# New key scores that wait longer for a page visit, and side jobs handed to PE with slack, in a planned decoder step

## The chip, the cores and the metric

The kernel runs on one core of a Trainium2 chip. The metric is the device time of one execution in microseconds (us). Before the change three runs took 855.38, 855.73 and 856.23 us; the median is 855.73. Engines are named as in the profile: PE is TensorE, PEld its weight load, DVE is VectorE, ACT is ScalarE, POOL is GpSimd, and SP is SyncE, which issues most DMA transfers.

## The reference

One decoder layer is computed in float32 for a prompt of 256 tokens and for 8 requests of 8 new tokens each, with 2048 cached tokens per request. One projection of the 320 rows feeds three groups of heads, and each group's output is multiplied by its own SiLU gate before the output projection and a LayerNorm:

```python
z = jnp.einsum('btd,dn->btn', h, w)          # one projection, cut into 13 parts
# A: sparse attention, 8 heads x 128: an indexer scores all keys, the best 256 or fewer are attended
s = jnp.einsum('bthd,btkhd->bthk', q, k_sel) * (DH_A ** -0.5)
# B: gated linear recurrence, 4 heads: S_t = diag(f_t) S_{t-1} + (1 - f_t) outer i_t, o_t = S_t^T q_t
# M: cross attention, 4 heads x 128, into 256 memory tokens per request
s = jnp.einsum('bthd,bnhd->bhtn', q, mk) * (DH_M ** -0.5)
y = jnp.einsum('btn,nd->btd', cat, w_out)
return _layernorm(ALPHA * h + y, ln_g, ln_b)
```

The cached keys and values lie in pages of 128 tokens, which a page table finds. The requests are handled in four pairs, p = 0 to 3; the keys of the 8 new tokens of each request are attended too.

## The kernel before, in words

**The matmuls.** Weights and activations are split into a high and a low part that PE multiplies at its fast float32 rate, so each product of a projection takes three matmuls (`xh` with `wh`, `xl` with `wh`, `xh` with `wl`). ACT casts the high part `wh` of a weight tile, DVE or POOL subtracts to get the low part `wl` (`prep`). A quantum of a projection is six matmuls. The projections (`wspec`, in the order of `PROJECTIONS`) run through the whole kernel; the memory projection is one of them; the output projection (`wo`) comes last.

**Page visits.** Keys and values come in units of two pages for each request of a pair. A visit (`unit`, line 722 and on) multiplies one or two units: `kv` rows are key scores with `qpad` as weights, `va` rows are values with the transposed probabilities `PT`. The weights of these matmuls have 32 columns, those of the projections 128. `units_now` takes two units together when the second is loaded too, and a single one when no projection part is about to be ready.

**Side jobs.** Everything else that PE does is in small generators in the list `bg`: attention scores, transposes, the recurrence (`hgrn`), the probabilities' transposes, cross attention (`cross_prompt`, line 1317). A generator stops at `yield need(...)`, which lists the tiles that it needs next, how many PSUM buffers (`ps`, 1 unless said), a `lag` and, for jobs whose weights have 32 columns too, a time `visit` that it may wait for a page visit. With `ps=0` the next step is not one of PE. There are three kinds of job with a visit time: the scores of the new tokens' own keys (`new_keys`, line 1201: `akS` with `qpad`, one job for each pair p), the recurrence's level scores (`kk, q, *lv`, time `HASTE`), and the state times queries of the decode part (`S0, q`, time `VISIT_WAIT`).

**The planner.** The order of all instructions is made when the program is built. `Plan` keeps, for each engine, the time up to which it is planned, and for each tile the time from which it can be read; each operation has a cost (`Engine.cost`) and each engine a latency. The loop at the end of the kernel (line 2115) goes on with the planned time `plan.now`: loads are issued on SP, weight parts prepared, finished projections evacuated, and `background` (line 2021) resumes side jobs whose needs are met. Then PE gets either a visit or a quantum of projection. `met` tells whether the tiles are ready: readable at `plan.now` or earlier, `lag` included. A job with a visit time is not resumed by `background` until that time has passed since it was first met; `join_visit`, called right behind a visit, resumes those that are met.

The engines execute what was put in their queues in that order, and wait on semaphores where a tile is not ready in reality. A planned time is no time of the chip, and none is used here.

Before the change the lines are:

```python
def need(*aps, ps=1, lag=0.0, visit=0.0):
    return (aps, ps, lag, visit)
...
        yield need(akS, st["qpad"], visit=VISIT_WAIT)
```

All operations are recorded by one helper, line 157, so the profile's rows are told apart by their tiles: `mB<-akS,qpad` are new key scores, `mB<-bp` level scores, `mA<-bp,t` with 128 columns out the decode state, `m.<-ident,t` transposes, `t<-t,s` of DVE the scaling of cross attention's probabilities.

Of the kernel before, what the change touches and what calls it, by code (L numbers as in the profile page):

```python
# [41 lines left out]
SOON = 0.4  # L42
LAG = 1.5
LAG2 = 0.8
VISIT_WAIT = 9.0
HASTE = 2.0
CALM = 4.0
# [172 lines left out]
        return (66 + n * f) / 960 + 0.055 * scalars  # L220


def need(*aps, ps=1, lag=0.0, visit=0.0):

    return (aps, ps, lag, visit)


@with_exitstack
def hymba_step(ctx: ExitStack, tc: tile.TileContext, I, O):
    nc = tc.nc  # L230
    plan = Plan()
    PE, ACT, DVE, POOL, SP = (Engine(plan, n, e) for n, e in (
        ("PE", nc.tensor), ("ACT", nc.scalar), ("DVE", nc.vector), ("POOL", nc.gpsimd), ("SP", nc.sync)))
# [22 lines left out]
    def free(*ts):  # L256
        for t in ts:
            e = live.get(t.tensor.name)
            if e:
                e[1] -= 1  # L260
                if e[1] == 0:
                    del live[t.tensor.name]
# [8 lines left out]
    def const(shape, name, dt=F32):  # L271
        return pool.tile(shape, dt, name=name, tag=name, bufs=1)

    def T(cols=NT, dt=F32):
        return new([128, cols], "t", dt)

    def T8():
        return new([128, 8], "s8")
# [9 lines left out]
    def n_free(which):  # L288
        return min(plan.n_free(which, 2), 2 - held[which])


    def PS(shape, which=None, dt=F32):
        if which is None:
            fa, fb = [(held[w] == 2, plan.slot_free(w, 2)) for w in ("mA", "mB")]
            which = "mA" if fa <= fb else "mB"
        return new(shape, which, dt, psum)
# [27 lines left out]
    akS = const([128, 8, NS], "akS")  # L324
# [26 lines left out]
    st = {}  # L351
# [101 lines left out]
    def pad_queries():  # L453
        yield from wait(("mq", 0))
        yield from room(1, "bp")
        st["mqpad"] = x = new([128, 8, 4, 32], "bp")
        POOL.memset(x, 0.0)
        for h in range(4):
            yield from wait(("mq", h))
            q = st.pop(("mq", h))  # L460
            yield need(q, ps=0)
            ACT.copy(x[:, :, h, 8 * h:8 * h + 8], q[:, 256:320].rearrange("p (b t) -> p b t", b=8))
            free(q)
        done.add("mqpad")
# [11 lines left out]
    def cat_put(c, part, cols, src, eng=None):  # L476
        out = cat_tile(c)[:, cols]
        if src.ndim > 2:
            out = out.rearrange("p (b q) -> p b q", b=src.shape[1])
        cat_left["p" if part == "p" else "s", c] -= 1  # L480
        if (c, part) in cat_seen:
            DVE.tensor_mul(out, out, src)
        else:
            cat_seen[c, part] = 1
            (eng or DVE.tensor_copy)(out, src)
# [17 lines left out]
    def gate(c, gates):  # L503
        for g, t in sorted(gates.items()):
            yield need(t, ps=0)
            cat_put(g, "p", slice(0, 256), t[:, 0:256])
            if g < 12:
                cat_put(g, "s", slice(256, 320), t[:, 256:320])
            else:
                for q in range(2):  # L510
                    s = slice(256 + 32 * q, 288 + 32 * q)
                    cat_put(g, ("s", q), s, t[:, s])
            free(t)
        done.add(("gate", c))
# [207 lines left out]
    def unit(n):  # L722
# [4 lines left out]
        if kind == "K":  # L727
# [12 lines left out]
            if u % 2:  # L740
                ps = st.pop("kv")
                plan.pinned.add(ps.tensor.name)
                bg.insert(0, [key_scores(p, u, ps), need(ps, ps=0)])
# [85 lines left out]
    def wait(*keys):  # L829
        while not all(k in done for k in keys):  # L830
            yield
# [85 lines left out]
    def idx_sample():  # L917
# [103 lines left out]
        for k, (sp, c, f, a) in enumerate(steps):  # L1021
            n = kk[0].shape[-1]
            yield need(ql, qh, *kk, ps=2, lag=LAG2)
            pd = [PS([128, 512]), PS([128, 512])]
# [176 lines left out]
    def new_keys(p):  # L1201

        yield from wait(("ak", 7))
        while p not in S:
            yield
        yield need(akS, st["qpad"], visit=VISIT_WAIT)
        ps = PS([128, NS])
        for hh in range(2):
            for h2 in range(2):
                for b, hp, g in GROUPS:  # L1210
                    h = 4 * hh + 2 * hp + h2
                    PE.matmul(ps[g:g + 32, :], st["qpad"][:, h, 2 * p + b, :], akS[:, h, :], start=hh == h2 == 0,
                              stop=hh == h2 == 1)
        plan.pinned.add(ps.tensor.name)
        yield need(ps, ps=0)
        plan.pinned.discard(ps.tensor.name)
        ACT.activation(S[p][:, PAST:], ps, AF.Copy, scale=QS)
        done.add(("new", p))
# [98 lines left out]
    def cross_prompt(h):  # L1317
        yield from wait("mem", ("mq", h), "attn")
        yield need(MQ[h], st["mkT"][h])
        ps = PS([128, 2, 256])  # L1320
        for tt in range(2):
            PE.matmul(ps[:, tt, :], MQ[h][:, 128 * tt:128 * tt + 128], st["mkT"][h], start=True, stop=True)
        s8 = T8()
        DVE.tensor_reduce(s8[:, 0:2], ps, axis=AX.X, op=OP.max)
        DVE.tensor_scalar(s8[:, 2:4], s8[:, 0:2], -QS, None, op0=OP.mult)
        free(MQ.pop(h), st["mkT"][h])
        P = [T(256), T(256)]
        yield need(s8, ps=0)
        for tt in range(2):
            ACT.activation(P[tt], ps[:, tt, :], AF.Exp, bias=s8[:, 2 + tt:3 + tt], scale=QS,  # L1330
                           accum_out=s8[:, 4 + tt:5 + tt])
        yield need(P[1], ps=0)
        DVE.reciprocal(s8[:, 6:8], s8[:, 4:6])
        for tt in range(2):
            DVE.tensor_scalar(P[tt], P[tt], s8[:, 6 + tt:7 + tt], None, op0=OP.mult)
        yield need(*P)
        pt = PS([128, 2, 2, 128])
        for nt in range(2):
            for tt in range(2):
                PE.transpose(pt[:, nt, tt, :], P[tt][:, 128 * nt:128 * nt + 128], ident)  # L1340
        free(*P)
        pts = [T(256), T(256)]
        for nt in range(2):
            ACT.copy(pts[nt], pt[:, nt].rearrange("p a b -> p (a b)"))
        yield need(*pts)
        po = PS([128, 256])
        for nt in range(2):
            PE.matmul(po, st["mv"][nt][h // 2][:, 128 * (h % 2):128 * (h % 2) + 128], pts[nt],
                      start=nt == 0, stop=nt == 1)
        cat_put(12 + h, "p", slice(0, 256), po, ACT.copy)  # L1350
        free(*pts)
        if h % 2:
            for nt in range(2):
                free(st["mv"][nt][h // 2])
# [10 lines left out]
    def hgrn():  # L1365
        lb, olb = lbt[:, 8:12], lbt[:, 12:16]
        yield from wait("idxdone", "pbias", "masks")
        for h in range(4):
# [184 lines left out]
            free(S2)  # L1553
            yield need(S0, q, visit=VISIT_WAIT)
            pq = PS([128, 2, 128])
# [457 lines left out]
    for g in (setup(), masks(), idx_head(), idx_sample(), attn_scores(), attn_values(), *[new_keys(p) for p in range(4)],  # L2013
              *[soft(p) for p in range(4)], hgrn(), pad_queries(), *[cross_prompt(h) for h in range(4)], split()):
        bg.append([g, None])
# [5 lines left out]
    def background():  # L2021
        rank = {"idx_load": 0, "idx_sample": 1, "idx_prompt": 1, "attn_scores": 2, "hgrn": 1, "xsoft": 1,
                "xextract": 1, "extract": 1, "key_scores": 0, "split": 1, "soft": 0, "attn_values": 1}
        for e in sorted(bg, key=lambda e: rank.get(e[0].__name__, 2)):
            for _ in range(4):
                if max(plan.t["DVE"], plan.t["ACT"]) > plan.now + (4, 3.5, 2)[int(rank.get(e[0].__name__, 2))]:
                    break
                if e[1]:
                    if not met(e[1]):
                        break  # L2030
                    if e[1][3] and nunit < len(punits) and plan.now < asked.setdefault(e[0], plan.now) + e[1][3]:
                        break
                if not resume(e) or e[1] is None:
                    break

    asked = {}

    def met(want):
        deps, nps, lag, _ = want
        return all(plan.avail(a) + lag <= plan.now for a in deps) and (not nps or n_free("mA") + n_free("mB") >= nps)  # L2040

    def resume(e):
        asked.pop(e[0], None)
        try:
            e[1] = next(e[0])
        except StopIteration:
            bg.remove(e)
            return False
        return True

    def join_visit():

        for e in list(bg):
            if e[1] and e[1][3] and met(e[1]):
                resume(e)

    def loads():
# [57 lines left out]
    while half < len(wspec) or bg or outq or later_in or pending or nunit < len(punits):  # L2115
        plan.now = max(plan.now, plan.t["PE"])
        loads()
        if pending and pending[0][0] is mem_values and has_room(4, spare=spare()):
            f, ps, _ = pending.pop(0)
# [8 lines left out]
        while pending and plan.avail(pending[0][1] if pending[0][2] == 3 else pending[0][1][-1]) <= plan.now \  # L2128
# [3 lines left out]
            f, ps, _ = pending.pop(0)  # L2132
# [139 lines left out]
```

## Time and profile before

| what | value |
|---|---|
| median of three runs | 855.73 us (855.38 to 856.23) |
| the profiled execution's own time | 855.43 us |
| its span, first to last instruction | 853.7 us |
| mean granted TensorE clock | 0.998 |
| HBM read | 256.50 MB |

The profile's first part gives the busy time of each engine and its share of the span, with the count of instructions. The list of waits names the engine and output tile that waited, who ended the wait, the time in total, how often, and the longest. In the timeline a row is the start, the time to the end of the row, the engine, the line, the operation with its output and inputs, the shape and the count; idle time of the engine ahead of it stands in brackets. Matmuls overlap in the timeline, so what one costs is the distance from its start to the next start. Some matmuls of float32 weights are recorded twice, once for each pass.

### The profile page before, as it was taken

How to read it: one execution, taken by the hardware profiler on the slowest of the kernel's cores; microseconds unless marked ns; L12 is line 12 of the kernel's file. 1: busy time of each engine (PE TensorE's matmuls, PEld its weight loads, DVE VectorE, ACT ScalarE, POOL GpSimd, SP SyncE). 2: the span in 40 equal slices, each digit the busy share in tenths (PEclk: the TensorE clock that was granted, in tenths of full speed). 3: DMA queues.
4: the chain of work that ended last, by engine and by line, in shares of the span. 5: the costliest groups of instructions: out<-in, count | busy, mean ns of one | idle time of the engine just before them, and what ended most of it. 6: DMA issues, size and time to landing. Idle time of an engine off the chain costs nothing.

```text
span 853.7 us, 19146 instructions
## 1 busy us (share of the span) xinstructions
PE 844.3 (99%) x6889; PEld 719.0 (84%) x6892; DVE 553.8 (65%) x1100; ACT 422.0 (49%) x908; POOL 325.4 (38%) x333
## 2 busy tenths in 40 slices
PE   9999999999999999999999999999999999999996
PEld 8999999877889898878778788787886889888885
DVE  7888897744897898654474456558545343953655
ACT  6454565553555543634544554555444353744432
POOL 0677562565634445331141214333311110713424
PEclk9999999999999999999999999999999999999999
DMA  8567557889999999999989999999999988756633
GB/s 342 171 190 226 158 172 253 281 308 412 375 388 395 336 322 366 398 367 399 390 321 412 407 352 393 398 370 412 338 411 396 350 329 285 279 172 199 195 99 123
DMA packets 83216, 266.49 MB, mean 312 GB/s; under 512 B 10481, under 2 KB 21170, under 8 KB 82482
## 3 DMA queue, kind: packets, MB, share of 16 engines
q1 hardware_dynamic: 82098, 263.18, 83.4%
q0 software_dynamic: 1024, 2.10, 0.8%
q8 instruction: 54, 0.88, 0.4%
q14 instruction: 40, 0.33, 0.1%
HBM read 256.50 MB, written 8.73 MB: 311 GB/s over the span
## 4 chain that ended last, share of the span: by engine, by line
PE 98%; DVE 1%; ACT 0%; issue 0%; DVEq 0%
PE pj L157 56%; PE mB L157 13%; PE va L157 10%; PE mA L157 10%; PE kv L157 8%; PE kv L1947 0%; DVE pg L157 0%; DVE t L157 0%; ACT t L157 0%; DVE wl L157 0%; DVE s L157 0%; DVEq L2258 0%; ACT wh L157 0%; DVE avn L157 0%; ACT kN L157 0%
## 5 line engine op out<-in xcount | busy, mean ns | idle before, releaser
L157 ACT CAST wh<-wr 128x512 fp32r<-128x512 f32 x334 | 204.5, 619 | 246.0 <-PE pj L157 186.8
L157 PE MATMUL pj<-xh,wh 128*128 128x320 f32 (+1 forms) x992 | 313.7, 316 | 0.0
L157 PE MATMUL pj<-xh,wl 128*128 128x320 f32 (+1 forms) x992 | 303.9, 306 | 0.0
L157 PE MATMUL pj<-xl,wh 128*128 128x320 f32 (+1 forms) x992 | 303.9, 306 | 0.0
L157 DVE TENSOR_TENSOR wl<-wr,wh 128x512 fp32r<-128x512 f32 x222 | 172.8, 786 | 183.4 <-ACT wh L157 169.6
L157 POOL TENSOR_TENSOR wl<-wr,wh 128x512 fp32r<-128x512 f32 x112 | 150.7, 1354 | 239.6 <-ACT wh L157 216.4
L157 PEld LDWEIGHTS pj<-xh,wh 128*128 128x128 f32 x992 | 186.7, 188 | 16.8 <-issue 13.0
L157 PEld LDWEIGHTS pj<-xl,wh 128*128 128x128 f32 x992 | 186.8, 188 | 1.3
L157 PEld LDWEIGHTS pj<-xh,wl 128*128 128x128 f32 x992 | 186.6, 188 | 0.0
L157 POOL TENSOR_TENSOR t<-t,t 128x256 f32<-128x256 f32 (+3 forms) x53 | 46.0, 869 | 121.3 <-ACT t L157 60.1
L157 PE MATMUL va<-pg,PT 128*32 128x512 f32 x456 | 58.4, 595 | 0.0
L157 PE MATMUL kv<-pg,qpad 128*32 128x256 f32 (+1 forms) x916 | 57.5, 380 | 0.0
L157 PEld LDWEIGHTS kv<-pg,qpad 128*32 128x32 f32 (+1 forms) x916 | 30.9, 110 | 20.5 <-issue 1.3
L157 PEld LDWEIGHTS va<-pg,PT 128*32 128x32 f32 x456 | 14.6, 109 | 30.4 <-issue 28.4
L157 DVE MAX8 PT<-PT 128x8 f32<-128x1032 f32 x32 | 39.5, 1234 | 0.5
L157 DVE MATCH_REPLACE8 PT<-PT 128x1032 f32<-128x1032 f32 x32 | 39.0, 1218 | 0.0
L157 POOL DMA_INDIRECT S<-in_ci,row x24 | 25.6, 1065 | 20.0 <-DVE row L157 10.5
L157 PE MATMUL mB<-t,wh 128*128 128x256 f32 x128 | 24.5, 289 | 0.0
L157 POOL TENSOR_TENSOR bp<-t,bp 128x128 f32<-128x128 f32 (+1 forms) x17 | 10.6, 625 | 36.0 <-ACT bp L157 36.0
L157 DVE TENSOR_TENSOR cat<-S,cat 64x512 fp32r<-64x512 f32 x24 | 19.2, 802 | 7.4 <-ACT cat L157 6.9
L157 POOL TENSOR_TENSOR t<-t,tabm 128x320 f32<-128x320 f32 x16 | 14.5, 906 | 24.4 <-DVE t L157 24.2
L157 POOL TENSOR_TENSOR xl<-cat,xh 128x256 fp32r<-128x256 f32 x12 | 12.5, 1060 | 24.9 <-ACT xh L157 24.9
(430 smaller groups left out, 1355.2 us busy)
## 6 DMA issues: line engine op xcount, KB each, us to landing
wr<-in_wt SPq DMA_DIRECT2D x124, 512.0 KB, 5.4
pg<-in_ck SPq DMA_DIRECT2D x114, 512.0 KB, 7.3
pg<-in_cv SPq DMA_DIRECT2D x114, 512.0 KB, 8.0
wr<-in_wo SPq DMA_DIRECT2D x36, 512.0 KB, 4.4
wr<-in_wm SPq DMA_DIRECT2D x16, 512.0 KB, 7.0
S<-in_ck SPq DMA_DIRECT2D x14, 512.0 KB, 6.5
S<-in_cv SPq DMA_DIRECT2D x14, 512.0 KB, 7.1
pg<-in_cXV SPq DMA_DIRECT2D x8, 512.0 KB, 8.1
```

The source lines that it names most:

```text
L157: res = f(*a, **k)
```

## The change: what it does

It adds a constant and changes five places:

```diff
+SLACK = 0.3
...
-def need(*aps, ps=1, lag=0.0, visit=0.0):
+def need(*aps, ps=1, lag=None, visit=0.0):
-    return (aps, ps, lag, visit)
+    return (aps, ps, lag if lag is not None else SLACK if ps and not visit else 0.0, visit)
...
-        yield need(akS, st["qpad"], visit=VISIT_WAIT)
+        yield need(akS, st["qpad"], visit=2 * VISIT_WAIT)
...
-        yield need(*P)
+        yield need(*P, lag=1.2)
         pt = PS([128, 2, 2, 128])
...
-    def met(want):
+    def met(want, now=None):
         deps, nps, lag, _ = want
-        return all(plan.avail(a) + lag <= plan.now for a in deps) and (...)
+        return all(plan.avail(a) + lag <= (now or plan.now) for a in deps) and (...)
...
     def join_visit():
         for e in list(bg):
-            if e[1] and e[1][3] and met(e[1]):
+            if e[1] and e[1][3] and met(e[1], max(plan.now, plan.t["PE"] - 0.4)):
                 resume(e)
```

A side job that needs PE and states neither a lag nor a visit time now gets a lag of 0.3: its tiles must have been readable for 0.3 us of planned time before PE is given the job. The transposes of the cross attention's probabilities `P` get 1.2. New key scores wait up to 18 instead of 9 us of planned time for a visit. And a visit takes the jobs whose tiles are readable 0.4 us before its own planned end, where before they had to be readable at its start. No operation is added or taken away by hand; all else that moves, moves because the planner places it otherwise. The order holds 5581 matmuls before and after.

Three places of the new order follow. The helper's line is 158 in the changed kernel.

On PE, the new key scores of pair p = 2; `pj` is a projection, `kv` a key visit, `cat,avn` the values of the prompt's attention. Before:

```order
L157 MATMUL pj_4217<-xh,wh_4204 128x320
L157 MATMUL pj_4217<-xl,wh_4204 128x320
L157 MATMUL pj_4217<-xh,wl_4205 128x320
L157 MATMUL mB_4309<-akS,qpad_411 32x64 x16
L157 MATMUL pj_4217<-xh,wh_4204 128x320
```

After:

```order
L158 MATMUL kv_4377<-pg_4247,qpad_411 32x256 x2
L158 MATMUL kv_4377<-pg_4206,qpad_411 32x256 x2
L158 MATMUL kv_4377<-pg_4247,qpad_411 32x256 x2
L158 MATMUL kv_4377<-pg_4206,qpad_411 32x256 x2
L158 MATMUL kv_4377<-pg_4247,qpad_411 32x256 x2
L158 MATMUL mA_4410<-akS,qpad_411 32x64 x16
L158 MATMUL mB_4433<-cat_469_3149,avn_4341 128x128 x3
```

The job stood between projection matmuls and now stands behind a key visit. So do those of pairs 0 and 1 together, and of pair 3. In the whole order there were 46 stretches of 32-column work and there are 42.

On PE, in the memory projection, the transposes of the last cross attention head (`ident,t`) and what follows them. Before:

```order
L157 MATMUL mB_8974<-ident,t_8868 128x128
L157 MATMUL mB_8974<-ident,t_8869 128x128
L157 MATMUL mB_8974<-ident,t_8868 128x128
L157 MATMUL mB_8974<-ident,t_8869 128x128
L157 MATMUL va_8553<-pg_8642,PT_8401 32x512 x2
```

After:

```order
L158 MATMUL mB_8961<-ident,t_8838 128x128
L158 MATMUL mB_8961<-ident,t_8839 128x128
L158 MATMUL mB_8961<-ident,t_8838 128x128
L158 MATMUL mB_8961<-ident,t_8839 128x128
L158 MATMUL pj_8974<-xh,wh_8818 128x320
```

A value visit followed the transposes, now a projection does; the visit comes behind the next 27 rows, among them the next jobs of this head and of the recurrence.

On ACT, at the hand-over to the output projection: the last four gates (`t<-t`), casts of weight parts (`wh`) and of the gated outputs (`qpad`, `xh`). Before:

```order
L157 ACTIVATE t_9771<-t_9771 128x320
L157 CAST wh_9785<-wr_9680 128x512
L157 CAST qpad_9711<-cat_469_3149 128x64
L157 CAST xh<-cat_469_3149 128x256
L157 CAST wh_9799<-wr_9680 128x512
```

After:

```order
L158 ACT_TABLE_LOAD
L158 ACTIVATE t_9469<-t_9469 128x320
L158 ACTIVATE t_9612<-t_9612 128x320
L158 ACTIVATE t_9684<-t_9684 128x320
L158 ACTIVATE t_9772<-t_9772 128x320
L158 CAST wh_9786<-wr_9682 128x512
L158 CAST wh_9796<-wr_9682 128x512
L158 CAST wh_9808<-wr_9730 128x512
L158 CAST wh_9818<-wr_9730 128x512
```

A table load has come in front of the gates, and four casts of weight parts follow them before the outputs are cast; before, casts of outputs stood in between. The order of ACT holds ten table loads now and held eight. From 652 matmuls before its end on, PE's order is the same in both. One visit of two key units, in the memory projection, has become two visits of one unit with 36 matmuls of the projection between.

More of the change, by code (lines that the diff above doesn't have):

```diff
@@ L2036, in hymba_step @@
     asked = {}
-    def met(want):
+    def met(want, now=None):
         deps, nps, lag, _ = want
-        return all(plan.avail(a) + lag <= plan.now for a in deps) and (not nps or n_free("mA") + n_free("mB") >= nps)
+        return all(plan.avail(a) + lag <= (now or plan.now) for a in deps) and (not nps or n_free("mA") + n_free("mB") >= nps)
     def resume(e):
```

## The prediction

> **What bounds the kernel now.** I read the page's shares and its chain first, then what PE waited for, then stretches of its timeline around the jobs that the change moves.
>
> ```profile
> PE 844.3 (99%) x6889; PEld 719.0 (84%) x6892; DVE 553.8 (65%) x1100; ACT 422.0 (49%) x908; POOL 325.4 (38%) x333
> ...
> PE 98%; DVE 1%; ACT 0%; issue 0%; DVEq 0%
> ```
>
> PE is busy for 99% of the span and carries 98% of the chain. What the whole kernel waited for on PE, in the list of waits:
>
> ```profile
> PE kv L1947 <- DVE t L157: 1.1, 1, 1.1
> PE mB L157 <- DVE t L157: 0.3, 1, 0.3
> ```
>
> The first is the warm-up. So PE's time is the number of its matmuls times their pace, plus the turns between kinds of matmul, plus very few stalls. The change keeps every matmul (the order has 5581 before and after), so it can only change turns and stalls. The profiled execution took 855.43 us with a span of 853.7; the median of the three runs is 855.73, 0.30 above it, and I add that 0.30 at the end. A measurement of this kernel tells about 0.2% from no change, 1.71 us: below 854.02 is faster, above 857.44 slower.
>
> **Turns.** A page visit and a few side jobs use weights of 32 columns (128*32 in the rows), the projections 128. The timeline of the new key scores of request pair p = 2, which stand alone among projections:
>
> ```profile
> 308.99 0.31 PE L157 MATMUL pj<-xh,wl 128*128 128x320 f32 x1
> 309.13 0.31 PE L157 MATMUL pj<-xh,wh 128*128 128x320 f32 x1
> 309.28 0.31 PE L157 MATMUL pj<-xl,wh 128*128 128x320 f32 x1
> 309.43 0.31 PE L157 MATMUL pj<-xh,wl 128*128 128x320 f32 x1
> 309.67 0.65 PE L157 MATMUL mB<-akS,qpad 128*32 128x64 f32 x32
> 310.25 0.41 PE L157 MATMUL pj<-xh,wh 128*128 128x320 f32 x1
> 310.50 0.30 PE L157 MATMUL pj<-xl,wh 128*128 128x320 f32 x1
> ```
>
> Matmuls overlap, so the pace is the distance of starts: 308.99 to 309.43 is three steps, 0.147 us each. From 309.43 to 310.50 it is 1.07; two projection matmuls are 0.29 of it, 0.78 are the job. The job's own matmuls are seen where two such jobs stand back to back:
>
> ```profile
> 247.94 0.65 PE L157 MATMUL mB<-akS,qpad 128*32 128x64 f32 x32
> 248.41 0.63 PE L157 MATMUL mA<-akS,qpad 128*32 128x64 f32 x32
> ```
>
> 248.41 - 247.94 = 0.47. The turn into 32 columns and back therefore costs 0.78 - 0.47 = 0.31 us. Behind a visit there is no such turn; here is the decode-state job (16 records, mA<-bp,t) behind the last step of a visit:
>
> ```profile
> 412.70 1.04 PE L157 MATMUL va<-avS,PT 128*32 128x512 f32 x8
> 413.56 0.62 PE L157 MATMUL mA<-bp,t 128*32 128x128 f32 x16
> 414.11 0.66 PE L157 MATMUL mB<-ident,S 128*128 128x128 f32 x4
> 414.61 0.60 PE L157 MATMUL mA<-ident,S 128*128 128x128 f32 x4
> ```
>
> The eight records of the visit take 0.86 to the job's start, two steps of 0.43, and nothing more. The recurrence's level scores, when alone, leave the same mark, a first projection matmul that takes 0.25 to the next:
>
> ```profile
> 390.44 0.41 PE L157 MATMUL pj<-xh,wh 128*128 128x320 f32 x1
> 390.69 0.30 PE L157 MATMUL pj<-xl,wh 128*128 128x320 f32 x1
> ```
>
> Counting stretches of 32-column work in the two orders gives 46 before and 42 now. All three stretches of new key scores that stood alone now stand behind a visit (-3); two of the four level scores stand next to a visit (-2); one visit of two key units is broken into two visits of one unit with 36 projection matmuls between (+1); one value visit is broken in both. Four turns at 0.31 are **-1.24 us**. The one price is measured for new key scores and taken for the others. The bounds: if the level scores' turn is free it is two turns, -0.62; if the broken key visit costs nothing it is five, -1.55.
>
> **The transposes of the cross attention.** The one stall on PE in the middle of the kernel:
>
> ```profile
> 655.50 1.29 POOL L157 TENSOR_TENSOR wl<-wr,wh 128x512 fp32r<-128x512 f32 x1 [2.45 <-ACT wh L157]
> ...
> 655.91 1.30 DVE L157 TENSOR_SCALAR t<-t,s 128x256 f32<-128x256 f32 x2
> ...
> 656.36 0.31 PE L157 MATMUL pj<-xh,wl 128*128 128x320 f32 x1
> ...
> 657.00 0.81 PE L157 MATMUL mB<-ident,t 128*128 128x128 f32 x4 [0.32 <-DVE t L157]
> ...
> 657.73 0.62 PE L157 MATMUL va<-pg,PT 128*32 128x512 f32 x2
> ```
>
> and the two DVE instructions in it, by tile (least, median, longest in ns):
>
> ```profile
> L157 DVE TENSOR_SCALAR t<-t,s x2: 340/686/1033, 655.9 to 656.9; 128x256 f32<-128x256 f32 x2
> ```
>
> One scaling took 340 ns, the other 1033, while POOL ran a 1.29 us subtraction until 656.79. PE, which had been handed the transposes, started them 0.64 after 656.36 instead of 0.147: 0.49 lost. The four then took 0.73 to the visit, against 0.50 for four in the rows above and 0.09 for the turn (309.67 - 309.43 - 0.147): 0.14 more. The stall is 0.63. The change hands these transposes over only when P has been ready for 1.2 us in the plan, so a delay of 0.69 (1033 - 340) is covered: **-0.63 us**; projections fill the time. The page "SBUF — State Buffer" of the Trainium skill (section "Who interferes with whom") says that a DVE instruction that meets a GpSimd one at the port they share is blocked for the whole of the other. The rows agree; by that rule a worst delay would be the full 1.29 and 0.09 of it would be left over the 1.2, and the sum would change by that 0.09 at most.
>
> **The slack of 0.3 us on the other side jobs.** No instruction is added. A side job is handed over up to one quantum of six projection matmuls (6 x 0.147 = 0.88) later, and ACT's and DVE's next steps with it. What hides this is that projections are there to run; the last side transposes now stand 24 projection matmuls nearer the end (3.5 us), with 636 matmuls still behind them. Cost nothing. It could remove stalls too, but the list of waits has no other on a side job, so no gain. The one further loss on PE, on a weight part:
>
> ```profile
> 735.82 3.35 POOL L157 TENSOR_TENSOR wl<-wr,wh 128x512 fp32r<-128x512 f32 x2 [0.80 <-ACT wh L157]
> ...
> 737.11 0.39 PE L157 MATMUL mA<-wh,xl 128*128 128x512 f32 x1
> ...
> 737.53 0.50 PE L157 MATMUL mA<-wl,xh 128*128 128x512 f32 x1
> 737.87 0.40 PE L157 MATMUL mB<-wh,xh 128*128 128x512 f32 x1
> ```
>
> Starts 0.42 and 0.34 apart against 0.23 here: 0.30 lost. It may go, stay or double: bounds -0.30 to +0.30, I take 0.
>
> **Two more table loads.** The order of ACT has 10 now, 8 before. One comes in front of the last four gates, at the hand-over to the output projection:
>
> ```profile
> 500.35 1.28 ACT L157 ACT_TABLE_LOAD   x1
> 501.64 1.55 ACT L157 ACTIVATE t<-t 128x320 f32<-128x320 f32 x4
> ...
> 730.35 1.55 ACT L157 ACTIVATE t<-t 128x320 f32<-128x320 f32 x4
> 731.81 0.61 ACT L157 CAST wh<-wr 128x512 fp32r<-128x512 f32 x1
> 732.32 0.24 ACT L157 CAST qpad<-cat 128x64 fp32r<-128x64 f32 x1
> ```
>
> ```profile
> 732.46 0.68 DVE L157 TENSOR_TENSOR wl<-wr,wh 128x512 fp32r<-128x512 f32 x1
> ...
> 734.16 0.39 PE L157 MATMUL mA<-wh,xh 128*128 128x512 f32 x1
> ...
> 734.62 0.39 PE L157 MATMUL mA<-wl,xh 128*128 128x512 f32 x1
> ```
>
> A load moves what follows by 501.64 - 500.35 = 1.29. The cast at 731.81 would end at 732.42 + 1.29 = 733.71, its low part on DVE at 734.39; PE wants it at 734.62 (this part feeds the quantum of 734.16). The next part goes to POOL: cast done 0.52 later, 734.23, then 1.29 to 1.68 (half of 3.35): 735.52 to 735.91, wanted at 734.62 + 1.36 = 735.98. Both just fit: nothing, bounds 0 and +0.3. The page "ScalarE: Activation LUTs" (section "What ACT_TABLE_LOAD costs") gives 2.66 us for a switch, with a drain of 1.38 us that the row at 501.64 does not show; that speaks against the change.
>
> **Sum.** 855.43 - 1.24 - 0.63 = 853.56; on the median's footing 853.86, **853.9 us**.
>
> **Rivals.** *The collision moves.* DVE and POOL trade some subtractions (DVE has four instructions more, POOL four fewer), and jobs that now join a visit are taken with 0.4 us to spare in the plan, less than the 0.69 that one collision cost. One or two stalls of 0.63 come back at other places: 854.5 to 855.1, I write 855.1. For it: the plan did not foresee the one collision; against: only one in the whole kernel had this effect, with no slack at all.
>
> *The transfers take the gain.* In the middle PE is no faster than the pages come (a stretch, the busy time of PE, PEld, DVE, ACT and POOL, the clock, the DMA share, GB/s):
>
> ```profile
> 520.00:540.00 20.00, 20.00 (x172) 17.19 (x172) 10.90 (x25) 10.74 (x24) 8.47 (x13) 1.00 1.02 386
> ```
>
> The DMA share is 1.02. If PE must wait for what it saved, only the late stall is gained: 855.1. Against: behind the last visit and side job the chain has 132 projection matmuls in a row, so pages may come later:
>
> ```profile
> 709.50 19.36 PE pj L157 x132
> ```
>
> *The table load at the hand-over.* If the load holds ACT for longer than 1.29 the low part at 734.39 is late; from 0.23 on PE waits. At twice 1.29 it would wait 1.06: 854.9. By the figure of the page on ScalarE it would be 1.14.
>
> *The SP queue, slower.* Loads of pages and weights wait in one queue in program order:
>
> ```profile
> SPq L157 <- DVE wl L157: 153.5, 82, 6.7
> ```
>
> Between the two single key units a page load can stand in front, its buffer freed only by the second unit, with a weight load behind it. PE then runs nothing while that unit waits; the 36 matmuls between the units (of the memory projection, so the pace of 0.147 is an estimate) give the size, 5.3. It decides where the weight load is issued behind that page load and its part is the next one wanted; 853.9 + 5.3 = 859.2. For it: a unit is taken singly when no projection part is ready. Against: in the traced execution no PE row waits for a DMA.
>
> That the jobs do not join is no rival: the order shows where they stand.
>
> **How the numbers follow.** Forecast 0.55, the moved collision 0.25, the transfers 0.08, the table load 0.06, the SP queue 0.06. The forecast lies 0.1 to 0.2 below the line of 854.02, and the runs before spread by 0.35 below and 0.50 above their median, so I give 0.05 of its 0.55 to "within". Faster 0.50, same 0.05 + 0.25 + 0.08 + 0.06 = 0.44, slower 0.06. The range goes from all bounds together, 853.9 - 0.31 - 0.30 and the spread of 0.35, 852.9, to the rivals within 0.2%, 855.1 and a stall of 0.30: 855.4.
>
> **What would show it.** Right: the new key scores directly behind kv rows with no first matmul of 0.25 behind them; four ident transposes of the cross attention without an idle entry; no new PE entry in the list of waits; the starts of the first output-projection matmul and of the last earlier by 1.9. Wrong: the matmul distance before a side job above 0.3 us in several places (collision), PE idle behind wr or pg landings (transfers), mA<-wl,xh late near 734 (table load), or a gap of some us between the single key units (queue).

## The result: slower by 0.8%, and the profile after

The changed kernel took 862.43 us (median of 4 runs, 861.34 to 863.49), the kernel before 855.75; the ratio is 1.0079 with a 95% interval of 1.0067 to 1.0092. The forecast of 853.9 had the wrong sign and the time lies above its range. The profiled execution is the longest of the four: 863.49 us, with a span of 861.7 against 853.7.

PE is still busy nearly all the time, but transfers stand in the chain that ended last, which before had none:

```profile
PE 845.5 (98%) x6892; PEld 721.9 (84%) x6892; DVE 551.8 (64%) x1104; ACT 424.9 (49%) x910; POOL 323.0 (37%) x329
...
PE 94%; DMA 3%; DVE 1%; ACT 1%; SPq 0%; issue 0%; DVEq 0%; ACTq 0%
```

The list of waits of PE (engine, tile, who ended the wait: us in total, times, longest) has new entries; the 1.1 is the warm-up, which was there before:

```profile
PE kv L158 <- DMA S<-in_ck: 3.4, 1, 3.4
PE mB L158 <- ACT t L158: 2.9, 2, 1.8
PE kv L1948 <- DVE t L158: 1.1, 1, 1.1
PE va L158 <- ACT PT L158: 0.6, 1, 0.6
PE mA L158 <- DVE s L158: 0.5, 1, 0.5
```

The longest is a key visit that waits for a page. The timeline shows it in the first of the two visits of a single unit: four records on one page, then nothing until the unit's other page, which was loaded into `S`, has landed. The same timeline shows the largest of the `mB` waits, at the transposes of the recurrence:

```profile
530.14 0.63 PE L158 MATMUL kv<-pg,qpad 128*32 128x256 f32 x4
534.12 0.41 PE L158 MATMUL kv<-S,qpad 128*32 128x256 f32 x2 [3.35 <-DMA S<-in_ck]
...
603.70 0.55 PE L158 MATMUL mB<-ident,t 128*128 128x128 f32 x3 [1.79 <-ACT t L158]
...
653.88 1.13 PE L158 MATMUL mB<-t,t 128*128 128x256 f32 x4 [1.11 <-ACT t L158]
```

The key visit's wait has a tail. In stretches of 2 us (busy time of PE, PEld, DVE, ACT, POOL, then the granted clock, the DMA share and GB/s) the clock falls to about half behind it:

```profile
532.00:534.00 2.00, 0.00 (x0) 0.00 (x0) 0.09 (x1) 0.00 (x0) 0.00 (x0) 1.00 1.04 406
534.00:536.00 2.00, 1.88 (x24) 1.32 (x26) 0.00 (x0) 0.00 (x0) 0.00 (x0) 0.64 1.04 412
536.00:538.00 2.00, 2.00 (x14) 0.91 (x6) 0.00 (x0) 0.00 (x0) 0.00 (x0) 0.51 1.02 408
538.00:540.00 2.00, 2.00 (x14) 1.79 (x13) 0.19 (x1) 0.90 (x3) 0.00 (x0) 1.00 1.03 398
```

That is 2 x 0.36 + 2 x 0.49 = 1.7 us more, so the one late page costs 3.35 + 1.7 = 5.05 in this execution. With the other waits (1.79, 1.11, 0.5, and 0.6 at the launch) the losses add up to 9.05; the span grew by 8.0, so about 1 us was gained elsewhere. The 0.6 at the launch need not be the change's: a kernel below that keeps the order of before (the dose) has 0.8 there.

**Why the page was late.** 20 us earlier the transfers had run dry. Over 8 us, first the kernel before, then the changed one:

```profile
506.00:514.00 8.00, 8.00 (x74) 7.32 (x64) 7.58 (x20) 3.19 (x7) 2.67 (x2) 1.00 0.90 314
```

```profile
506.00:514.00 8.00, 8.00 (x126) 6.34 (x125) 6.80 (x20) 4.22 (x11) 2.11 (x2) 1.00 0.43 124
```

190 GB/s less for 8 us are 1.52 MB that were not moved; at the 406 GB/s of the stretch before the landing they take 3.7 us, the size of the wait. PE does not feel it at once, since the pages already loaded keep it busy. SP had nothing in flight because a weight load at its head waited for DVE's low part to free the weight buffer. SP's longest wait in this place, before and after:

```profile
SPq L157 <- DVE wl L157: 5.4, 2, 4.7
```

```profile
SPq L158 <- DVE wl L158: 9.2, 1, 9.2
```

And DVE was late because of ACT. In the timeline of the kernel before, the norm of the recurrence's second head (its sum `mB<-t,onesm` on PE, `t<-mB,eps` on ACT, then on DVE) goes ahead of the second group's gates (table load, four `t<-t`):

```profile
497.67 0.70 PE L157 MATMUL mB<-t,onesm 128*128 128x320 f32 x2
...
498.46 0.53 ACT L157 ACTIVATE t<-mB,eps 128x320 f32<-128x320 f32 x1 [1.69 <-PE mB L157]
...
501.56 0.68 DVE L157 TENSOR_TENSOR wl<-wr,wh 128x512 fp32r<-128x512 f32 x1
...
502.27 0.34 SPq L157 DMA_DIRECT2D wr<-in_wt  x1
```

In the changed kernel the gates go first, with a load of their table and another to come back:

```profile
500.89 1.28 ACT L158 ACT_TABLE_LOAD   x1
...
501.44 0.70 PE L158 MATMUL mB<-t,onesm 128*128 128x320 f32 x2
...
502.18 1.55 ACT L158 ACTIVATE t<-t 128x320 f32<-128x320 f32 x4
503.75 1.28 ACT L185 ACT_TABLE_LOAD   x1
505.05 0.53 ACT L158 ACTIVATE t<-mB,eps 128x320 f32<-128x320 f32 x1
...
506.11 0.55 DVE L158 SCALAR_TENSOR_TENSOR t<-mB,eps,t 128x320 f32<-128x320 f32 x1 [3.65 <-ACT t L158]
...
507.64 1.28 POOL L158 TENSOR_TENSOR wl<-wr,wh 128x512 fp32r<-128x512 f32 x1
507.72 1.55 DVE L158 SCALAR_TENSOR_TENSOR t<-t,t 128x320 f32<-128x320 f32 x1 [1.05 <-POOL t L158]
509.19 1.28 DVE L158 TENSOR_TENSOR wl<-wr,wh 128x512 fp32r<-128x512 f32 x2
509.90 0.34 SPq L158 DMA_DIRECT2D wr<-in_wt  x1
```

The norm's sum is done on PE at 502.14, but ACT, busy with the gates and the two loads since 500.89, takes it only at 505.05; before, ACT took it 0.1 us after PE was done (498.37 and 498.46). DVE's instructions behind the norm wait with it, one of them then runs for 1.55 beside POOL, and the weight load goes out at 509.90. The number of loads at this place is two in both kernels; only their position against the norm changed.

### The profile page after: what moved, and what is told of

It reads as the page before. It is cut to its first block, busy times and chain, and to the rows that moved or that the text cites. A ratio compares the mean times of both kernels' runs of the same rounds, so it can differ in the third digit from the quotient of the medians.

```text
span 861.7 us, 19135 instructions
## 1 busy us (share of the span) xinstructions
PE 845.5 (98%) x6892; PEld 721.9 (84%) x6892; DVE 551.8 (64%) x1104; ACT 424.9 (49%) x910; POOL 323.0 (37%) x329
## 4 chain that ended last, share of the span: by engine, by line
PE 94%; DMA 3%; DVE 1%; ACT 1%; SPq 0%; issue 0%; DVEq 0%; ACTq 0%
PE pj L158 54%; PE mB L158 12%; PE va L158 10%; PE mA L158 10%; PE kv L158 8%; DMA S<-in_ck 1%; DMA pg<-in_ck 1%; DMA S<-in_first 1%; ACT t L158 0%; DVE t L158 0%; SPq L158 0%; DVE pg L158 0%; DVE wl L158 0%; ACT wh L158 0%; ACT xh L158 0%
## 5 line engine op out<-in xcount | busy, mean ns | idle before, releaser
L158 DVE TENSOR_TENSOR wl<-wr,wh 128x512 fp32r<-128x512 f32 x222 | 168.8, 766 | 181.6 <-ACT wh L158 167.8
L158 ACT ACTIVATE S<-kv 128x512 f32<-128x512 f32 x16 | 9.5, 595 | 25.5 <-PE kv L158 25.5
```

Source lines behind the costliest of these rows:

```text
L158: res = f(*a, **k)
```

## The experiments

Two theories were to be told apart. Theory A: the chain just told, ACT's order, DVE, the weight load at the head of SP, dry transfers, a late page. Theory B: many small misses by jobs that the slack, the lag and the joining place badly. In these comparisons "before" took 855.9 us. A ratio is that of the run to the kernel before, with its 95% interval.

**One part alone, and all but one.** First only the doubled time of the new key scores:

```diff
-        yield need(akS, st["qpad"], visit=VISIT_WAIT)
+        yield need(akS, st["qpad"], visit=2 * VISIT_WAIT)
```

> Only the doubled visit time of the new key scores; no slack, no lag of 1.2, visits join as before. Theory A (the queue): the doubled time alone moves the gates of the second group in front of the recurrence's norm on ACT, the two table loads hold the norm, DVE's low part behind the norm and with it the weight load on SP, pages come late, a key visit waits 3 us or more and PE's clock falls behind it. Expected 860 to 863 us, with an SP wait near 9 us before 510 and a PE wait for S<-in_ck. Theory B (many small misses: the slack, the lag and the earlier joining place jobs badly): this part alone only joins key scores to visits, 855 to 856 us, no PE wait over 1 us.

Measured 860.16 (ratio 1.0049, 1.0035 to 1.0063). The order on ACT at 500 is that of the changed kernel, SP waits 9.0 us and the key visit 3.3:

```profile
PE kv L157 <- DMA S<-in_ck: 3.3, 1, 3.3
...
PE mA L157 <- ACT t L157: 0.5, 1, 0.5
```

Theory A is borne out, and the waits on `mB` are not there. Why the planner puts the gates ahead of the norm when key scores wait longer is not shown. Then the rest without this part:

> The change without the doubled visit time: slack, lag of 1.2 and earlier joining stay. Theory A: the hold on SP and the key visit's wait are not there; no turns are saved (46 stretches as before), the transposes' stall of 0.63 goes: 855.0 to 855.8 us. Theory B: the stalls stay with the slack and the joining: 858 to 860 us.

Measured 855.55 (0.9998, 0.9989 to 1.0007). PE's list of waits has the warm-up alone. So slack, lag and joining do no harm that can be measured by themselves. All but the slack (`lag=0.0` as the default again):

> The change without the slack of 0.3 us. Theory A with the late stalls from the slack: the key visit's wait near 530 stays, the waits near 601 and 652 (1.95 and 1.28 us) go: 858.5 to 860.5 us. If they come with the new key scores or the joining, they stay: 861.5 to 863 us.

Measured 860.19 (1.0052, 1.0039 to 1.0066), 2.2 below the whole change. The page's wait is as long; the waits on `mB` are gone:

```profile
PE kv L157 <- DMA S<-in_ck: 3.4, 1, 3.4
...
PE pj L157 <- ACT t L157: 0.8, 1, 0.8
```

Some 4.3 us belong to the doubled time and 2.2 to the slack together with it. The waits bear out the second: 1.79 + 1.11 went and 0.8 came, 2.1 in all. Last the lag of the cross attention's transposes alone:

```diff
-        yield need(*P)
+        yield need(*P, lag=1.2)
```

> Only the lag of 1.2 for the cross attention's transposes. By the prediction's term the stall of 0.63 us goes and nothing else moves: 855.0 to 855.5 us. Rival (the work behind the transposes comes later and gives it back): 855.7 to 856.3 us.

Measured 854.82 (0.9990, 0.9981 to 0.9999), 0.2 below the range expected and the only kernel here whose whole interval lies below before. No wait on `mB<-ident,t` is left.

**The chain on ACT, taken apart.** The same order on all engines, without the two table loads at 500; the gates of the second group lack their SiLU. The lines that leave out the second load and keep the plan's times are not shown:

```diff
                 for g in sorted(GT):
-                    ACT.activation(GT[g], GT[g], AF.Silu)
+                    ACT.activation(GT[g], GT[g], AF.Silu if c != 7 else AF.Copy)
...
```

> The changed kernel in the same order on every engine, but the gates of the second group are left as they are (an identity in place of SiLU), so the two table loads around them are not there: 2.57 us less on ACT ahead of the norm. Theory A: the SP wait of 9.2 us falls by 2.6 to about 6.6, the key visit's wait of 3.4 to 0.8 or less, and the slow clock behind it (1.7) goes: 857.5 to 859 us. Theory B, or a hold of SP from another cause: the key visit waits as before, 861.5 to 863 us.

Measured 857.56 (1.0021, 1.0011 to 1.0031), 4.9 below the changed kernel. No page is waited for; the `mB` waits are still there:

```profile
PE mB L158 <- ACT t L158: 2.9, 2, 1.8
PE va L158 <- ACT PT L158: 1.2, 2, 0.7
...
PE mA L158 <- DVE s L158: 0.2, 1, 0.2
```

SP's wait is 4.0, less than the 6.6 expected. In the timeline the norm's second product on DVE takes 0.49, where the changed kernel's took 1.55 beside POOL's low part:

```profile
505.13 0.49 DVE L158 SCALAR_TENSOR_TENSOR t<-t,t 128x320 f32<-128x320 f32 x1 [1.06 <-POOL t L158]
...
506.25 0.34 SPq L158 DMA_DIRECT2D wr<-in_wt  x1
```

The weight load went out 3.65 us earlier (509.90 - 506.25): 1.06 is the meeting with POOL (1.55 - 0.49), the other 2.59 are the two table loads (1.29 + 1.30). So the hold was made by both.

The other way round: the order by another rule. `ev_gate`'s function for the second group is held while a norm is under way.

```diff
             ACT.activation(sq, po, AF.Square)
+            st["norm"] = True
...
             ACT.activation(y, y, AF.Exp, scale=-0.5)
+            st["norm"] = False
...
-                and (pending[0][0] not in late or "attn" in done) and out_ready(pending[0][0]):
+                and (pending[0][0] not in late or "attn" in done and not (st.get("norm") and late.index(pending[0][0]) == 0)) and out_ready(pending[0][0]):
```

> The changed kernel, with the second group's gates held back until the norm of the recurrence's head has been put on ACT. Theory A: the low part on DVE comes about 4 us earlier, the SP wait is 5 us or less, no PE wait for S<-in_ck, no slow clock; the other waits (601, 652, 333) may stay: 856 to 858 us. Theory B: the time stays at 861.5 to 863 us, since the small misses stay.

Measured 860.40 (1.0051, 1.0037 to 1.0065): a miss by 2.4. The weight cast still stood behind the gates, SP waited 6.9, and the key visit 1.5. With the gates held back until the next call of `prep`, so that the cast too goes first:

> The changed kernel, with the second group's gates held back until the norm and the next weight cast are on ACT, the order that ACT had before the change at this place. Theory A: SP's wait there is about 4.7 us as before, no key visit waits for a page, no slow clock; the late transposes and scores (1.95 and 1.28 us) stay: 856.5 to 857.8 us. If something else than ACT's order holds the pages, a wait of 1.5 us or more stays and the time is over 859.

Measured 859.44 (1.0039, 1.0026 to 1.0053), another miss, by 1.6. SP's wait at 500 is 4.6 as expected and the order alone gives back 3.0 of the loss, but the visit still waits 0.7 + 0.2, and the waits on `mB` (3.0) stay. A second weight load holds SP later, in front of the `S` pages; SP's waits from 512 to 531 in this kernel:

```profile
SPq L158 <- POOL wl L158: 4.2, 2, 3.8
SPq L158 <- DVE t L158: 0.4, 1, 0.4
```

So the order at 500 is not the only thing that can make this visit wait: a later weight load that holds SP in front of its page can do it too.

**A dose in the kernel before.** Its order is left alone; ACT is made late at the same place by repeating an operation that changes nothing.

```diff
+            for _ in range(8 if h == 1 else 0):
+                ACT.raw.activation(y, ps, AF.Ln, bias=eps[:, 0:1])
             ACT.activation(y, ps, AF.Ln, bias=eps[:, 0:1])
```

> The kernel before, same order, with the logarithm of the second head's norm on ACT done eight times over (the result is the same): about 4 us more on ACT at the place where the changed kernel has its gates. Theory A: SP's wait there grows from 4.7 to between 8 and 9 us, the transfers run dry, a visit waits 1.5 to 3 us and PE's clock falls: 858 to 861 us. Theory B (the hold on SP is harmless, other places make the loss): 855.5 to 856.3 us.

Measured 861.17 (1.0063, 1.0049 to 1.0077), a little above the range. SP's waits there and PE's longest wait, also longer than expected, in an execution of 863.35:

```profile
SPq L157 <- DVE wl L157: 10.2, 2, 9.6
```

```profile
PE kv L157 <- DMA pg<-in_ck: 4.3, 1, 4.3
```

About 4.5 us of ACT work (eight logarithms, 4.45 in the trace), on an engine that is busy half the time, make the kernel 5.3 us longer. With three repeats:

> As the first dose, with three logarithms in place of eight: about 1.5 us more on ACT ahead of the second head's norm in the kernel before. Theory: the SP wait of 4.7 us grows to about 6.2, and from the points measured (4.0 and 4.7 without a wait of a visit, 6.9 with 1.5, 9.2 with 3.4, 9.6 with 4.3) a visit waits about 1 us: 856.6 to 857.8 us. Rival (the pages have slack until SP has waited some 7 us): 855.5 to 856.2 us.

Measured 857.17 (1.0015, 1.0006 to 1.0024); SP waited 6.0 and a visit 1.3. There is next to no slack: some 1.6 us on ACT (1.65 in the trace) cost 1.3. And eight repeats at the fourth head (`h == 3`):

> The kernel before with the logarithm done eight times ahead of the fourth head's norm: the same 4 us on ACT at another place, late in the kernel. Theory (the price is that of the place: transfers at their limit and a weight load in front of the pages on SP): without such a queue there the time stays within 0.6 us of before, 855.5 to 856.5. Rival (ACT's delay itself is what costs): 858 to 861 us as in the first dose.

Measured 856.77 (1.0013, 1.0004 to 1.0022), 0.3 above the range expected; PE has no new wait of over 0.2, and where the 0.9 us come from is open. It is the place that makes most of the price, 5.3 us or 0.9.

Put together, all in the traced executions: SP's longest wait near 500, the longest that a weight load made on SP later (512 to 531), and the wait of the key visit behind both:

| kernel | SP near 500, us | SP later, us | key visit waits, us |
|---|---|---|---|
| better kernel (below) | 4.0 | 3.8 | 1.5 |
| gates without loads | 4.0 | 2.7 | 0 |
| cast first | 4.6 | 3.8 | 0.7 and 0.2 |
| before | 4.7 | 2.6 | 0 |
| small dose | 6.0 | 2.0 | 1.3 |
| norm first | 6.9 | 3.7 | 1.5 |
| without two POOL subtractions (below) | 7.5 | 1.1 | 3.2 |
| slack taken out | 8.7 | 0.6 | 3.4 |
| doubled time alone | 9.0 | 0.2 | 3.3 |
| changed | 9.2 | 0 | 3.4 |
| dose | 9.6 | 3.5 | 4.3 |

From 6.0 on the visit's wait grows with the first column; below that a visit waited only where the later wait was 3.8. Before and the two doses have the visit of two units, the others the single ones, so the rows are no exact scale.

**The late transposes.** In the changed kernel DVE runs slowly just ahead of the recurrence's transposes at 603.70; `t<-mB` is the copy that empties the PSUM buffer they need:

```profile
599.12 3.00 POOL L158 TENSOR_TENSOR wl<-wr,wh 128x512 fp32r<-128x512 f32 x2 [2.80 <-ACT wh L158]
...
599.60 1.38 DVE L158 TENSOR_TENSOR wl<-wr,wh 128x512 fp32r<-128x512 f32 x1 [1.48 <-ACT wh L158]
...
600.90 1.58 DVE L158 SCALAR_TENSOR_TENSOR t<-t,ngt,t 128x320 f32<-128x320 f32 x1
...
602.82 0.75 DVE L158 COPY t<-mB 128x256 f32<-128x256 f32 x2
```

The two subtractions on POOL were taken out, the order otherwise kept; the products lack two low parts:

```diff
+            if (i, j) in ((126, 1), (127, 1)):
+                WL[i][j] = hi
...
+            else:
+                TT(OP.subtract, lo[:, 0:w], raw, hi[:, 0:w].bitcast(F32))
```

> The changed kernel in the same order, without the two subtractions on POOL that run from 599.12 to 602.12 (the matmuls with those two low parts take the high parts instead, so the products lack their low parts). Theory: DVE's subtraction (1.38) and its three-operand product (1.58) took 0.69 and 0.55 elsewhere and met POOL there, the copies that free the PSUM buffer came 1.7 late; without POOL the wait of 1.95 us near 601 falls to 0.3 or less, 860.3 to 861.3 us. Rival (DVE's queue is too long there anyway): the wait stays over 1.5, 861.5 to 863 us.

The wait is gone, and DVE runs at its usual pace:

```profile
599.22 0.69 DVE L158 TENSOR_TENSOR wl<-wr,wh 128x512 fp32r<-128x512 f32 x1 [1.48 <-ACT wh L158]
599.83 0.55 DVE L158 SCALAR_TENSOR_TENSOR t<-t,ngt,t 128x320 f32<-128x320 f32 x1
...
600.73 0.74 DVE L158 COPY t<-mB 128x256 f32<-128x256 f32 x2
```

The median of 861.43 (1.0068, 1.0055 to 1.0080), just above the range, is 1.0 below that of the changed kernel, with intervals that overlap: the cause of this wait is shown, its 1.8 us in the medians is not. The traced spans differ by 2.0 (861.7 and 859.7), with the same 1.7 us of slow clock in both. The wait at 653.88 stays (1.1); its cause is open. The Trainium skill, "SBUF — State Buffer", section "Who interferes with whom", has DVE blocked by a GpSimd instruction at a port that they share; 0.69 beside 1.38 and 0.55 beside 1.58 agree.

**An attempt at a better kernel.** Cast first, as above, and two jobs of the last heads handed over later:

```diff
-            yield need(f, bi)
+            yield need(f, bi, lag=2.5 if h == 3 else None)
...
-        yield need(MQ[h], st["mkT"][h])
+        yield need(MQ[h], st["mkT"][h], lag=1.5 if h == 3 else None)
```

> As the kernel with norm and cast ahead of the gates, and two jobs of the last heads handed over later: the transposes of the recurrence's inputs with a lag of 2.5, the cross attention's scores with 1.5. Theory: with the page wait and both late stalls gone the gain of the turns (two to four at 0.31) is left: 853.5 to 855.0 us. Rival: other jobs are late in their place: 855.5 to 857.5 us.

Measured 858.16 (1.0024, 1.0013 to 1.0034). Both late jobs are on time, the page is late by 1.5 (POOL's low part held SP for 3.8 again), and another job is late:

```profile
PE kv L158 <- DMA S<-in_ck: 1.5, 1, 1.5
PE mA L158 <- ACT t L158: 1.3, 1, 1.3
```

The rival's mechanism was right, though the time lies 0.7 above its range too: a new order has its own late places.

## Why the prediction was wrong, step by step

**What bounds the kernel.** That PE's time is matmuls, turns and stalls holds, but for the pace: it halved for a while behind the long wait, 1.7 us that no term had. The step that failed is the use of the list of PE's waits as a catalogue of what could stall: what the new order moves on ACT, DVE and SP was put at nothing, since no PE row waited for it before. In its place the runs showed gates that moved ahead of a norm on ACT, a weight load held on SP until 509.90, and a late page that cost 5.05 in the traced execution; the same order without the two table loads there is 4.9 shorter. The list says what is late now, not by how little the rest is on time. The small dose shows that little: about 1.6 us more on ACT, and a visit waits 1.3.

**Turns, -1.24.** The three new key scores did join visits. What that gave is not measured by itself. In the traced executions the losses are about 1 us more than the growth of the span in the changed kernel, and 1.4 more with the doubled time alone (3.3 of page, 1.7 of clock, 0.5 and 0.4 of small waits against 4.5); so something of this size was gained, in the first case with the old stall of 0.63 in it, but its split is open. The 0.31 was measured for one job and stands for that.

**Transposes, -0.63.** Right: with the lag alone the wait is gone and the ratio's interval, 0.9981 to 0.9999, holds the 0.9993 that this term gives; the interval is too wide to settle the size.

**Slack, nothing.** Wrong in company. Without the doubled time it costs nothing that can be measured, with it 2.2 us. Behind that stand a wait of 1.79, made by a meeting of POOL and DVE, and one of 1.11 whose cause is open. "Projections fill the time" covers a job that is handed over late; it does not cover a job that is handed to PE and then finds its PSUM buffer not yet emptied.

**Two more table loads, nothing.** At the hand-over, where the load was priced, no PE wait appeared. But the loads were only counted. The pair that both orders have, around the gates at 500, had moved ahead of the norm; this was to be read in the order of ACT, and with DVE's and SP's queues behind it, it is the larger part of the loss.

**The rival on SP's queue** (859.2, chance 0.06) was the nearest: a held load in SP's queue that keeps others back. Its place and condition were others: not a page load between the two single units, but a weight load 20 us earlier that starved the first of them. That its 5.3 is near 3.35 and 1.7 of slow clock is luck: it was the time of the 36 matmuls between the units. What spoke against it, "no PE row waits for a DMA", is the reason that failed; the 4.7 us that SP already waited at 500, with the DMA share at 1.02 from 490 to 500, spoke for it.

**The other rivals.** *The collision moves* came true as well, at nearly three times its price (1.79 against 0.63), but in a job that the slack moved, not one that joined a visit. *The transfers take the gain* was in the right stretch, where the transfers are at their limit; that they took the gain of the turns is not shown. The rivals were weighed as if only one could come; two came together, and the range had no room for that.

## What to carry to other kernels

An engine that is half idle can still carry the critical path, through a queue: before pricing a move on it, follow what is queued behind the moved instruction on each engine in turn, down to the load that waits for a buffer. In a stretch where the transfers run at their limit, ask how long the loading queue already waits there; here nearly each further microsecond came back later as a wait of PE, and PE's own list of waits in the kernel before did not show it. Compare the order of instructions that both versions have, not only their number.

## What the runs showed of the hardware

A wait of PE can cost half as much again. Behind the 3.35 us without a matmul the clock was 0.64 and 0.51 for 4 us, 1.7 us lost. The kernels with the doubled time alone (a wait of 3.3) and without the two POOL subtractions (3.2) lost the same 1.7. In the dose, with a wait of 4.28, it fell while PE still waited, then stayed at 0.50, and 3.4 us were lost in all:

```profile
520.00:522.00 2.00, 0.00 (x0) 0.00 (x0) 1.97 (x2) 0.00 (x0) 0.00 (x0) 0.58 1.03 418
522.00:524.00 2.00, 1.60 (x16) 0.90 (x20) 1.96 (x7) 1.19 (x4) 0.79 (x1) 0.50 1.04 419
```

With the slack taken out a wait of 3.4 us, over at 533.2, left it at full rate:

```profile
534.00:536.00 2.00, 2.00 (x24) 1.27 (x16) 0.00 (x0) 0.00 (x0) 0.00 (x0) 1.00 1.04 414
```

The Trainium skill, "TensorE: Matmul & The Clock Gate", section "What's actually happening", states a half rate after an idle window of about 3.4 us, and that the window runs freely; waits of nearly this length with different ends agree with it. The tail need not be in every execution: of the four of the changed kernel three have a mean clock of 0.996, and the shortest, of 861.34 us, has 0.998; a stretch of 3.4 us at half the rate lowers the mean over 862 us by that 0.002.
